# Score products of differential attention: the lo part of the queries laid on both halves of the rows

## The chip, the cores and the metric

One Trainium2 chip (trn2), one of its cores. The metric is the device time of one execution in microseconds (us); lower is better. A measurement of this kernel gives the median of several runs.

## What is computed

The reference is a decoder layer over 1024 positions of 1024 channels. The change touches the scores of its first part, differential attention with 4 heads. Each head has two score sets (c = 0, 1) with 64 channels each, two softmaxes, and the difference of the two weighs the values:

```
sc = jnp.einsum("bhcqd,bhckd->bhcqk", q_blk, k).astype(jnp.float32) * scale
sc = jnp.where(mask, sc, -jnp.inf)
p = jax.nn.softmax(sc, axis=-1)
a = p[:, :, 0] - lam * p[:, :, 1]
return jnp.einsum("bhqk,bhkv->bhqv", a.astype(v.dtype), v)
```

Beside it run a convolution branch (width 31, LayerNorm, swish), cross-attention into 256 memory tokens and a gated feed-forward part with its own convolution.

## The kernel before, in words

TensorE multiplies in fp32r, a rounded form of float32. To keep the precision of float32 each operand is split into hi (rounded) and lo (the rest), and a product is made of several: `mm3` (lines 198 to 200) does hi x lo, lo x hi and hi x hi, on 128 rows each.

The stages follow each other: input projection, attention, output projection, cross-attention, feed-forward part. In the attention stage the score products have only 64 channels to sum over. So the kernel lays K by 128 rows: `ks[c]` holds the hi part of the keys of set c on one half of the rows and the lo part on the other half. `qd[c]` holds the hi part of the queries on both halves, so one product of 128 rows gives q_hi x k_hi + q_hi x k_lo. The lo part of the queries, `ql`, holds set 0 on rows 0 to 63 and set 1 on rows 64 to 127; one product of 64 rows gives q_lo x k_hi. The term q_lo x k_lo is left out.

`qk_split` (line 667 on) makes these tiles once per head. It casts K and Q to hi on ScalarE and subtracts for lo on VectorE (lines 220 and 221 in `split`), and the puts (`put`, line 676) copy halves of rows to where they belong. Every put is a transfer of 64 rows x 4 KB from SBUF to SBUF, issued on the queue of SyncE (SP), which also issues the loads of weights (line 171) and the stores of memory keys and values (`kv_dr`, lines 635 and 655). Of a head's tiles the first `nq` come from pool Q (8 tiles), the rest from pool R (26 tiles).

The attention loop goes over 32 units, four heads with eight query blocks of 128 in the order `QBS = [7, 0, 6, 1, 5, 2, 4, 3]`. A unit of query block qb has (qb + 1) x 128 keys. Up to 512 keys (small unit) both sets go into one PSUM tile, and the scores of both stand together; above that (large unit) each set is a part of its own with a PSUM tile of its own, cut into pieces of at most 512 columns. After the products of a part comes the mask product (line 705). Then VectorE takes the row maximum (line 715), ScalarE the exponential (line 721), VectorE combines the two sets (lines 741 to 745); two steps later TensorE transposes (line 759), four steps later it weighs the values (line 772). Between these, TensorE works on products of the memory keys and values (`mm3` with 256 columns), the filler. VectorE also works through the convolution (line 371).

TensorE's order is the order in which the program is written (`manual_schedule`), and it works through it in order. The order of the other engines and of SP's queue comes from a scheduler that plans with its own costs. `qk_split` of head h + 1 is appended after step 4 of head h, and the casts come in step 5:

```
            if step % 8 == 4 and step < 24:
                lanes.append(qk_split(step // 8 + 1))
```

The first head is split before the loop.

Of the kernel before, what the change touches and what calls it, by code (L numbers as in the profile page):

```python
# [10 lines left out]
F32R = mybir.dt.float32r  # L11
# [46 lines left out]
def hybrid_block_kernel(ctx: ExitStack, tc: tile.TileContext, xT, memT, pos, vecs, lams, ropec,  # L58
                        wi, wv, wo, wq, wkv, wc, wu, wd, gfin, outT, outB):
    nc = tc.nc  # L60
# [15 lines left out]
    def nm(s):  # L76
        cnt[0] += 1
        return f"{s}_{cnt[0]}"

    def R():  # L80
        return pt.tile([P, S], F32R, tag="t", name=nm("r"))

    def Q(dt=F32):
        return pq.tile([P, S], dt, tag="q", name=nm("q"))
# [4 lines left out]
    def BIG():  # L89
        return big[0].tile([P, S], F32, tag="big", name=nm("big"))  # L90
# [16 lines left out]
    def f(ap):  # L107
        return ap.bitcast(F32)
# [76 lines left out]
    def need(kind, m, ahead=None):  # L185
        if ahead is None:
            ahead = 1
        load_to(index[(kind, m)] + ahead)
        return prepped.pop((kind, m))
# [15 lines left out]
    def bs(b):  # L205
        return slice(b * P, (b + 1) * P)

    def proj(w, xs, ks=None, kmajor=True):

        ks = list(range(KT)) if ks is None else list(ks)  # L210
        ps = BIG()
        loops = [(k, h) for k in ks for h in range(2)] if kmajor else [(k, h) for h in range(2) for k in ks]
        for k, h in loops:
            mm3(ps[:, hs(h)], (w[0][:, bs(k)], w[1][:, bs(k)]), xs(k, h), k == ks[0], k == ks[-1])
        return ps

    def split(src, hi, lo, scale=None):

        if scale is None:
            nc.scalar.copy(out=hi, in_=src)  # L220
            nc.vector.tensor_tensor(out=lo, in0=src, in1=f(hi), op=ALU.subtract)  # L221
        else:
            nc.scalar.mul(hi, src, scale)
            nc.vector.scalar_tensor_tensor(out=lo, in0=src, scalar=scale, in1=f(hi), op0=ALU.mult, op1=ALU.subtract)
# [262 lines left out]
    qk = [None] * 8  # L487
# [22 lines left out]
    with tc.manual_schedule(engines={mybir.EngineType.PE}):  # L510
        w, w2 = need("in", 12), need("in", 8, 0)
        ps, ps2 = BIG(), BIG()
# [26 lines left out]
    for m in in_order[3:]:  # L539
        w = need("in", m)  # L540
        ps = proj(w, xs_in)
# [125 lines left out]
    def qk_split(h):  # L667


        nq = (0, 2, 2, 4)[h]  # L670
        t = [Q(F32R) if i < nq else R() for i in range(5)]
        ks, qd, ql = t[:2], t[2:4], t[4]
        rows = (slice(0, 64), slice(64, P))

        def put(dst, src):
            nc.sync.dma_start(out=f(dst), in_=f(src))

        kh, kl = R(), R()
        split(qk[4 + h], kh, kl)
        for c in range(2):  # L680
            put(ks[c][rows[c]], kh[rows[c]])
            put(ks[c][rows[1 - c]], kl[rows[c]])
        yield
        qh = R()
        split(qk[h], qh, ql)
        for c in range(2):
            put(qd[c][rows[0]], qh[rows[c]])
            put(qd[c][rows[1]], qh[rows[c]])
        yield
        hl[h] = ks, qd, ql  # L690

    def scores(u, cs):

        h, qb = u["h"], u["qb"]
        nk = (qb + 1) * P
        ks, qd, ql = hl[h]
        cuts = [0, 384, 640] if nk == 640 else [*range(0, nk, HALF), nk]
        for n0, n1 in zip(cuts, cuts[1:]):
            for c in cs:
                rows = slice(64 * c, 64 * c + 64)  # L700
                nc.tensor.matmul(u["ps"][c][:, n0:n1], ql[rows, bs(qb)], ks[c][rows, n0:n1], start=True, stop=False)  # L701
            for c in cs:
                nc.tensor.matmul(u["ps"][c][:, n0:n1], qd[c][:, bs(qb)], ks[c][:, n0:n1], start=False, stop=n1 < nk)  # L703
        for c in cs:
            nc.tensor.matmul(u["ps"][c][:, nk - P:nk], identb, maskb, start=False, stop=True)
# [18 lines left out]
    def start_unit(h, qb):  # L724
        nk = (qb + 1) * P
        if (h, qb // 4) not in s0:
            s0[(h, qb // 4)] = small(4, "s0", 4)
        u = {"h": h, "qb": qb, "sums": small(2, "sums", 6), "nmx": small(2, "nmx", 6)}
        if nk <= HALF:
            both = BIG()  # L730
            t = T()
            u.update(both=both, ps=[both[:, hs(0)], both[:, hs(1)]], p=[t[:, :nk], t[:, HALF:HALF + nk]])
        else:
            u.update(both=None, ps=[None, None], p=[None, None])
        return u
# [172 lines left out]
    for _ in qk_split(0):  # L908
        pass
    with tc.manual_schedule(engines={mybir.EngineType.PE}):  # L910
# [3 lines left out]
        for step in range(n + LW):  # L914
# [4 lines left out]
            u = None  # L919
            if step < n:  # L920
                u = start_unit(*plan[step])
                units.append(u)
                if u["both"] is not None:
                    scores(u, (0, 1))
                    maxima(u, None)
                else:
                    u["ps"][0] = span(u)
                    scores(u, (0,))
                    maxima(u, 0)
# [16 lines left out]
            if u and u["both"] is None:  # L946
                u["ps"][1] = span(u)
                scores(u, (1,))
                maxima(u, 1)
                u["p"][1] = T()[:, :(u["qb"] + 1) * P]  # L950
                expo(u, 1)
# [4 lines left out]
            if step % 8 == 4 and step < 24:  # L956
                lanes.append(qk_split(step // 8 + 1))
# [37 lines left out]
    for m in range(8):  # L995
        res = Q()
        nc.scalar.dma_start(out=res, in_=xT[bs(m), :])
        if m < 2:
            ps = two[m]
        else:  # L1000
            ps = proj(need("out", m), xs_out)
# [190 lines left out]
    for m in range(8):  # L1192
        ps = proj(need("co", m), xs_co) if m > 1 else co[m]
# [401 lines left out]
```

## Time and profile before

| what | before |
|---|---|
| median of 3 runs | 1430.73 us (1429.91 to 1436.02) |
| the profiled execution | 1430.6 us |
| its span | 1428.7 us |
| PE busy | 1398.4 us (98%) |
| DVE (VectorE) busy | 1059.6 us (74%) |
| ACT (ScalarE) busy | 570.6 us (40%) |
| POOL (GpSimd) busy | 200.5 us (14%) |

The span is what the profile covers of an execution; the rest lies around it. PE is TensorE's products, PEld its weight loads, which may run beside products. A product's record is longer than its share of the array, since products follow each other in a pipeline: the distance from start to start tells what one costs, not its length. SPq is SP's queue; a row there is the time of issuing a transfer, not of the transfer.

### The profile page before, as it was taken

What the parts mean: (1) busy time and instruction counts of PE and PEld (TensorE: products, weight loads), DVE (VectorE), ACT (ScalarE), POOL (GpSimd) and SP (SyncE); (2) the same over time, 40 slices, a digit from 0 to 9 for tenths busy, and PEclk for the clock granted to TensorE, in tenths of its full rate; (3) what the DMA queues carried; (4) which work ended last, traced back from release to release, by engine and by line L of the source; (5) the groups of instructions that cost most, each with busy time, mean ns of one, the idle gap of its engine ahead of it and who ended that gap; (6) DMA issues with size and microseconds to landing.
All of it is one profiled execution on the core that took longest, in us unless ns stands there. A gap on an engine that the chain in (4) does not pass through costs nothing.

```text
span 1428.7 us, 17463 instructions
## 1 busy us (share of the span) xinstructions
PE 1398.4 (98%) x6709; PEld 1148.1 (80%) x6709; DVE 1059.6 (74%) x1377; ACT 570.6 (40%) x1015; POOL 200.5 (14%) x169
## 2 busy tenths in 40 slices
PE   9999999999999999999989999999999989999998
PEld 6888887778777888888878888788888878888886
DVE  7899998878855424454688888888888887656636
ACT  6211224667773223343464443444443442211213
POOL 0000000013110000000114234343334400000000
PEclk9999999999999999999999999999999999999999
DMA  6142135523405421112431222222222274323103
GB/s 230 34 103 63 56 103 144 159 83 103 119 31 171 163 101 59 63 42 74 148 111 59 74 74 89 79 84 74 89 75 89 89 308 163 108 70 118 44 1 118
DMA packets 51620, 141.55 MB, mean 99 GB/s; under 512 B 6608, under 2 KB 8912, under 8 KB 51536
## 3 DMA queue, kind: packets, MB, share of 16 engines
q1 hardware_dynamic: 45040, 123.65, 26.1%
q10 hardware_dynamic: 6496, 16.78, 3.7%
q8 instruction: 53, 0.87, 0.3%
q14 instruction: 31, 0.25, 0.1%
HBM read 101.51 MB, written 28.41 MB: 91 GB/s over the span
## 4 chain that ended last, share of the span: by engine, by line
PE 65%; DVE 15%; issue 7%; ACT 7%; POOL 4%; DMA 2%; SPq 0%; POOLq 0%; ACTq 0%; DVEq 0%
PE big L198 15%; PE big L199 15%; PE big L200 15%; DVE q L1323 4%; POOL t L1178 4%; ACT q L1321 3%; PE big L703 2%; PE tb L772 2%; PE big L701 2%; PE bk L198 1%; PE bk L200 1%; PE bk L199 1%; DVE wu L221 1%; DVE q L1342 1%; PE mb L198 1%
## 5 line engine op out<-in xcount | busy, mean ns | idle before, releaser
L199 PE MATMUL big<-r,wlo 128*128 128x512 f32 x624 | 243.2, 390 | 0.6 <-DVE wlo L182 0.6
L200 PE MATMUL big<-r,whi 128*128 128x512 f32 x624 | 243.0, 389 | 0.0
L198 PE MATMUL big<-r,whi 128*128 128x512 f32 x560 | 219.0, 391 | 2.0 <-DVE r L304 1.0
L181 ACT CAST whi<-raw 128x1024 fp32r<-128x1024 f32 x58 | 61.3, 1056 | 205.2 <-PE big L200 169.6
L199 PEld LDWEIGHTS big<-r,wlo 128*128 128x128 f32 x624 | 117.2, 188 | 24.7 <-DVE wlo L182 0.9
L200 PEld LDWEIGHTS big<-r,whi 128*128 128x128 f32 x624 | 117.2, 188 | 24.5
L1427 DVE TENSOR_TENSOR t<-t,big 128x1024 f32<-128x1024 f32 x70 | 85.3, 1219 | 62.1 <-PE big L200 62.0
L1323 DVE SCALAR_TENSOR_TENSOR q<-q,vec,q 128x1023 f32<-128x1023 f32 x88 | 112.5, 1280 | 20.5 <-ACT q L1321 20.4
L198 PEld LDWEIGHTS big<-r,whi 128*128 128x128 f32 x560 | 105.2, 188 | 25.3 <-DVE r L304 1.9
L198 PE MATMUL big<-r,r 128*128 128x512 f32 x312 | 121.8, 390 | 0.3 <-DVE t L1427 0.3
L199 PE MATMUL big<-r,r 128*128 128x512 f32 x312 | 121.5, 390 | 0.0
L200 PE MATMUL big<-r,r 128*128 128x512 f32 x312 | 121.5, 389 | 0.0
L198 PE MATMUL ub<-r,wu 128*128 128x512 f32 x302 | 118.6, 393 | 1.2 <-ACT half L1278 1.2
L200 PE MATMUL ub<-r,wu 128*128 128x512 f32 x302 | 117.6, 389 | 0.0
L199 PE MATMUL ub<-r,wu 128*128 128x512 f32 x302 | 117.6, 389 | 0.0
L1178 POOL TENSOR_TENSOR t<-uraw 128x512 f32<-128x512 f32 x22 | 48.6, 2210 | 387.7 <-DMA uraw<-in_wu_dram 166.9
L198 PE MATMUL ub<-r,t 128*128 128x512 f32 x228 | 91.2, 400 | 9.5 <-ACT half L1278 4.8
L199 PE MATMUL ub<-r,t 128*128 128x512 f32 x228 | 90.2, 396 | 0.0
L200 PE MATMUL ub<-r,t 128*128 128x512 f32 x228 | 90.0, 395 | 0.0
L371 DVE SCALAR_TENSOR_TENSOR cv<-t,vec,cv 128x511 f32<-128x511 f32 (+14 forms) x120 | 83.8, 739 | 0.0
L181 ACT CAST r<-raw 128x1024 fp32r<-128x1024 f32 x22 | 23.0, 1049 | 135.4 <-PE big L198 134.7
L182 DVE TENSOR_TENSOR wlo<-raw,whi 128x1024 fp32r<-128x1024 f32 x58 | 70.7, 1220 | 4.8 <-ACT whi L181 4.7
(333 smaller groups left out, 3010.5 us busy)
## 6 DMA issues: line engine op xcount, KB each, us to landing
uraw<-in_wu_dram SPq DMA_DIRECT2D x88, 256.0 KB, 2.9
z_dr<-q SPq DMA_DIRECT2D x22, 512.0 KB, 2.6
raw<-in_wd_dram SPq DMA_DIRECT2D x22, 512.0 KB, 3.7
t<-z_dr SPq DMA_DIRECT2D x22, 512.0 KB, 4.6
raw<-in_wkv_dram SPq DMA_DIRECT2D x16, 512.0 KB, 3.7
raw<-in_wi_dram SPq DMA_DIRECT2D x14, 512.0 KB, 3.6
r<-r SPq DMA_DIRECT2D x16, 256.0 KB, 6.1
kv_dr<-r SPq DMA_DIRECT2D x8, 512.0 KB, 3.5
```

The lines of the kernel that those rows point to most:

```text
L181: nc.scalar.copy(out=hi, in_=raw)
L182: nc.vector.tensor_tensor(out=lo, in0=raw, in1=f(hi), op=ALU.subtract)
L198: nc.tensor.matmul(out, wh, xl, start=start, stop=False, **kw)
L199: nc.tensor.matmul(out, wl, xh, start=False, stop=False, **kw)
L200: nc.tensor.matmul(out, wh, xh, start=False, stop=stop, **kw)
L371: nc.vector.scalar_tensor_tensor(out=y[:, i:], in0=x[:, :n2 - i], scalar=t, in1=y[:, i:], op0=ALU.mult, op1=ALU.add)
L701: nc.tensor.matmul(u["ps"][c][:, n0:n1], ql[rows, bs(qb)], ks[c][rows, n0:n1], start=True, stop=False)
L703: nc.tensor.matmul(u["ps"][c][:, n0:n1], qd[c][:, bs(qb)], ks[c][:, n0:n1], start=False, stop=n1 < nk)
L1178: nc.gpsimd.tensor_tensor(out=out, in0=a, in1=b, op=ALU.add)
L1321: nc.scalar.mul(t, u, tp[2])
L1323: nc.vector.scalar_tensor_tensor(out=t[:, d:], in0=u[:, :S - d], scalar=tp[2 - d], in1=t[:, d:], op0=ALU.mult, op1=ALU.add)
L1427: nc.vector.tensor_tensor(out=h2[m], in0=h2[m], in1=ps, op=ALU.add)
```

## The change

`ql` becomes two tiles like `qd`: `ql[c]` holds the lo part of the queries of set c on both halves of the rows. The lo part is first computed into a tile of its own, `qlo`, and four more puts per head copy it. All score products take 128 rows, so the lo product now gives q_lo x k_hi + q_lo x k_lo. In small units the lo and the hi product of set 0 stand ahead of those of set 1, where the two lo products stood first.

```diff
         nq = (0, 2, 2, 4)[h]
-        t = [Q(F32R) if i < nq else R() for i in range(5)]
-        ks, qd, ql = t[:2], t[2:4], t[4]
+        t = [Q(F32R) if i < nq else R() for i in range(6)]
+        ks, qd, ql = t[:2], t[2:4], t[4:]
...
-        qh = R()
-        split(qk[h], qh, ql)
+        qh, qlo = R(), R()
+        split(qk[h], qh, qlo)
         for c in range(2):
-            put(qd[c][rows[0]], qh[rows[c]])
-            put(qd[c][rows[1]], qh[rows[c]])
+            for r in rows:
+                put(qd[c][r], qh[rows[c]])
+                put(ql[c][r], qlo[rows[c]])
...
             for c in cs:
-                rows = slice(64 * c, 64 * c + 64)
-                nc.tensor.matmul(u["ps"][c][:, n0:n1], ql[rows, bs(qb)], ks[c][rows, n0:n1], start=True, stop=False)
-            for c in cs:
+                nc.tensor.matmul(u["ps"][c][:, n0:n1], ql[c][:, bs(qb)], ks[c][:, n0:n1], start=True, stop=False)
                 nc.tensor.matmul(u["ps"][c][:, n0:n1], qd[c][:, bs(qb)], ks[c][:, n0:n1], start=False, stop=n1 < nk)
```

In the new file the lo product is line 701, the hi product line 702 and the mask product line 704; later lines move up by one.

What the scheduler makes of it stands in the order of the programs. SP's queue at head 0, before: `r_1761` and `r_1762` are ks, `r_1763` and `r_1764` are qd of set 0 and 1, `raw` is a weight load.

```order
L676 DMA r_1761<-r_1766 64x1024
L676 DMA r_1762<-r_1766 64x1024
L676 DMA r_1761<-r_1767 64x1024
L676 DMA r_1762<-r_1767 64x1024
L676 DMA r_1763<-r_1774 64x1024 x2
L676 DMA r_1764<-r_1774 64x1024 x2
L171 DMA raw_1904<-in_wkv_dram 128x1024
```

The same place in the new program; `r_1765` and `r_1766` are ql of set 0 and 1.

```order
L676 DMA r_1761<-r_1767 64x1024
L676 DMA r_1762<-r_1767 64x1024
L676 DMA r_1761<-r_1768 64x1024
L676 DMA r_1762<-r_1768 64x1024
L676 DMA r_1763<-r_1775 64x1024 x2
L171 DMA raw_1910<-in_wkv_dram 128x1024
L676 DMA r_1765<-r_1776 64x1024 x2
L676 DMA r_1764<-r_1775 64x1024
L676 DMA r_1766<-r_1776 64x1024
L676 DMA r_1764<-r_1775 64x1024
L676 DMA r_1766<-r_1776 64x1024
L171 DMA raw_1967<-in_wkv_dram 128x1024
```

Four puts are added, and one weight load now stands between qd and ql of set 0. In heads 1 and 2 the order is the same from the second put of qd of set 0 on.

SP's queue at head 3, before: `q_3383` and `q_3384` are ks, `q_3385` and `q_3386` are qd.

```order
L676 DMA q_3383<-r_3388 64x1024
L655 DMA kv_dr<-r_2839 128x1024
L676 DMA q_3384<-r_3388 64x1024
L676 DMA q_3385<-r_3416 64x1024
L676 DMA q_3383<-r_3389 64x1024
L676 DMA q_3384<-r_3389 64x1024
L676 DMA q_3385<-r_3416 64x1024
L676 DMA q_3386<-r_3416 64x1024 x2
L171 DMA raw_4185<-in_wo_dram 128x1024
```

The same place in the new program; `q_3403` and `q_3404` are qd, `r_3405` and `r_3406` are ql.

```order
L676 DMA q_3401<-r_3407 64x1024
L676 DMA q_3402<-r_3407 64x1024
L655 DMA kv_dr<-r_2857 128x1024
L676 DMA q_3403<-r_3435 64x1024
L676 DMA q_3401<-r_3408 64x1024
L676 DMA q_3402<-r_3408 64x1024
L676 DMA q_3403<-r_3435 64x1024
L676 DMA q_3404<-r_3435 64x1024 x2
L676 DMA r_3405<-r_3436 64x1024 x2
L676 DMA r_3406<-r_3436 64x1024 x2
L171 DMA raw_4209<-in_wo_dram 128x1024
```

Here all puts of ql stand behind those of qd. On PE the order of the products is the same but for the small units, where L701 of set 1 now stands behind the hi product of set 0.

## Rows read from the trace of the kernel before

**Rows 1.** Busy time by stretch: the attention stage (us, PE, PEld, DVE, ACT, POOL, PEclk).

```profile
236.90:410.00 173.10, 166.31 (x1095) 130.13 (x1095) 140.67 (x272) 119.96 (x321) 25.97 (x55) 1.00 0.40 117
```

**Rows 2.** Waits, 228 to 412 us, of DVE and SP: total us, times, longest.

```profile
DVE s L715 <- PE big L705: 28.0, 29, 2.6
...
SPq L171 <- DVE wlo L182: 52.1, 8, 20.2
```

**Rows 3.** PE in order of time at head 1's first part: start us, us.

```profile
288.52 0.28 PE L199 MATMUL mb<-r,wlo 128*128 128x256 f32 x1
288.64 0.28 PE L200 MATMUL mb<-r,whi 128*128 128x256 f32 x1
288.85 0.49 PE L701 MATMUL big<-q,r 64*128 64x512 f32 x1
289.27 0.50 PE L703 MATMUL big<-q,r 128*128 128x512 f32 x1
...
290.48 0.23 PE L705 MATMUL big<-maskb,identb 128*128 128x128 bf16 x1
```

**Rows 4.** PE in order of time in the value projection, products of 512 columns.

```profile
225.68 0.39 PE L199 MATMUL bk<-whi,r 128*128 128x512 f32 x1
225.90 0.39 PE L200 MATMUL bk<-whi,r 128*128 128x512 f32 x1
```

**Rows 5.** PE in order of time, a small unit of 128 keys in head 1.

```profile
295.08 0.33 PE L701 MATMUL big<-q,r 64*128 64x128 f32 x2
...
295.62 0.29 PE L705 MATMUL big<-maskb,identb 128*128 128x128 bf16 x2
```

**Rows 6.** The last two puts (L676) of heads 0 to 3 on SP: issue, landing.

```profile
L676 SPq DMA_DIRECT2D r<-r x2: 913/1031/1149, 234.1 to 235.1; - x2
...
DMA to landing us min/median/max: 6.0/6.1/6.2
...
L676 SPq DMA_DIRECT2D r<-r x2: 891/1197/1503, 281.6 to 283.2; - x2
...
DMA to landing us min/median/max: 6.1/6.3/6.4
...
L676 SPq DMA_DIRECT2D r<-r x2: 556/811/1066, 325.5 to 326.2; - x2
...
DMA to landing us min/median/max: 6.4/6.4/6.4
...
L676 SPq DMA_DIRECT2D q<-r x2: 622/744/867, 372.5 to 373.2; - x2
...
DMA to landing us min/median/max: 4.8/5.1/5.3
```

**Rows 7.** PE in order of time: first products of the first two parts of the heads.

```profile
239.00 0.50 PE L703 MATMUL big<-r,r 128*128 128x512 f32 x1 [1.59 <-DMA r<-r]
...
242.56 0.50 PE L701 MATMUL big<-r,r 64*128 64x512 f32 x1
...
293.18 0.49 PE L701 MATMUL big<-q,r 64*128 64x512 f32 x1
...
331.72 0.50 PE L701 MATMUL big<-q,r 64*128 64x512 f32 x1
...
335.76 0.50 PE L701 MATMUL big<-q,r 64*128 64x512 f32 x1
...
376.25 0.49 PE L701 MATMUL big<-q,r 64*128 64x512 f32 x1
...
379.87 0.49 PE L701 MATMUL big<-q,r 64*128 64x512 f32 x1
```

**Rows 8.** Busy time by stretch around two idle spells of PE, columns as in rows 1.

```profile
739.10:743.30 4.20, 4.17 (x10) 3.30 (x11) 4.01 (x4) 2.93 (x6) 2.97 (x2) 0.50 0.18 64
1161.50:1165.70 4.20, 0.07 (x1) 0.00 (x0) 4.13 (x6) 2.77 (x3) 0.00 (x0) 1.00 1.03 417
1166.60:1170.00 3.40, 3.40 (x10) 2.62 (x9) 3.36 (x3) 2.72 (x3) 0.00 (x0) 0.50 1.03 411
```

## The prediction

> **What bounds the kernel now.** I read the table of stretches first, then TensorE (PE) in order of time, then the puts and the waits. The attention stage takes 173.1 us of the span, with PE busy 166.3 us and VectorE 140.7 [rows 1]. PE's instructions stand in a fixed order, so this stage ends when PE has gone through them; VectorE idles 32 us in it, and 28.0 us of that is the row maximum (L715) waiting for score products [rows 1, 2].
>
> Busy does not mean at full rate. In the timeline of one score part (head 1, 1024 keys, four products of 512 columns) the reader is to see starts: L701 to L703 takes 0.42 us, and first L701 to mask product (L705) 1.63 us for four products [rows 3]. Products of the same 512 columns that use all 128 rows one after another start 0.22 to 0.23 us apart elsewhere [rows 4]. So each change between 64 rows (L701) and 128 rows (L703) costs some 0.2 us. The change into the first L701 shows too: it comes 0.21 us after a product of 256 columns, where such products follow each other after 0.12 [rows 3].
>
> **What the change removes.** With 128 rows everywhere no product changes the row count. A part of 1024 keys took 0.21 + 1.63 = 1.84 us and takes 0.12 + 4 x 0.227 = 1.03: 0.8 saved. The surplus hangs on the changes, not on the columns, so I take 0.8 for all 32 large parts (4 heads, 4 query blocks, 2 score sets): 25.6 us. The 16 small units (up to 512 keys) gain little: there the two 64-row products run side by side, two of 128 columns together in 0.33 us [rows 5], and this overlap is lost. The one shown takes 0.54 + 0.21 now and 4 x 0.12 + 0.12 then, 0.15 saved; I take 0.2 each, 3.2 us (bounds 0 and 0.3). Together PE saves **28.8 us**, 7.2 in each head. No instruction is added on PE, ScalarE or VectorE; the added lo x lo terms ride in rows that were empty.
>
> A rule of the Trainium skill speaks against this: its page TensorE: Matmul & The Clock Gate (Part 3: Packing small matmuls — row/col tiling) says that a weight load overlaps a running product only when it goes to other rows of the array. By it no 128-row product could hide its load and the large parts would gain nothing. The row contradicts it, products of 128 rows with new weights at 0.227 us [rows 4]; by the rule the 25.6 us would be nothing, and it is a rival below.
>
> **What the change adds.** Four transfers per head (L676, 64 rows x 4 KB), all on SP's one queue, and all behind the split of the queries. The first part of a head now needs its two ql puts as well as its two qd puts. In the order of heads 0 to 2, a weight load, then ql of set 0, then the four puts of set 1 stand behind qd of set 0; in head 3 ql stands behind all qd. So ql of set 0 is complete one transfer after the last put of the old kernel (two in head 3), and ql of set 1 four transfers later (two in head 3).
>
> The old last puts landed at 241.3, 289.3, 332.6 and 378.5 us (issue plus landing: 235.1 + 6.2, 283.2 + 6.1, 326.2 + 6.4, 373.2 + 5.3), each 0.7 to 1.3 after the put before it [rows 6]. I take **1.1 us a transfer** (bounds: 0.55, were two halves to travel together, and 1.35). The weight load of 512 KB isn't priced apart in a row; I take the same, bounds 0.55 and 2.2. That puts ql of set 0 at 242.4, 290.4, 333.7 and 380.7.
>
> Old starts of the first parts: 238.6 effectively (the L703 at 239.00 had waited 1.59 for puts, less 0.42), 288.85, 331.72, 376.25 [rows 3, 7]. PE must wait for every head. How long follows from a chain: the puts of head h+1 start when the split in step 5 of head h is cast, behind six large parts and three small ones (6 x 0.8 + 3 x 0.2 = 5.4 us saved by then); the last 1.8 us saved before a head begins only lengthen its wait.
> - Head 0: starts 3.8 late. The second part followed the first by 242.56 - 238.6 = 4.0 us, now 3.2, but its puts come 4.4 after the first's: 1.2 more. At the cast: 3.8 + 1.2 - 5.4 = 0.4 early.
> - Head 1: ql at 290.4 - 0.4 = 290.0; PE is there at 288.85 - 0.4 - 1.8 = 286.65: **waits 3.35**. Start 1.15 late; second part (4.33 apart, now 3.5) 0.9 more; at the cast 3.4 early.
> - Head 2: ql at 330.3, PE at 326.5: **waits 3.8**; start 1.4 early; second part 1.2 more; at the cast 5.6 early.
> - Head 3: ql at 375.1, PE at 368.85: **waits 6.2**; start 1.2 early; the second part (3.6 apart, now 2.8) needn't wait, its puts come 2.2 after. Then 7.2 saved: 8.4 early.
>
> So of 28.8 us some 20 go into waits and 8.4 stay. Two costs come off.
> (a) PE's clock. After 4.2 us without work the granted clock was 0.50, 1.2 of 2.4 GHz, for 3.4 us; and after another such spell 10 products took 4.2 us at 0.50, which is 10 x 0.227 = 2.3 at full clock [rows 4, 8]. So about 1.8 us per wait that long. The new waits are 5.5 (head 0: 242.4 less 236.9, the start of the old first product, 0.5 + 1.59 before 239.00), 3.35, 3.8 and 6.2. In heads 0 to 2 the wait of the second part swallows 1.2, 0.9, 1.2 of it. All four: 0.6 + 0.9 + 0.6 + 1.8 = 3.9; only the longest two: 2.4. I take 3.2.
> (b) VectorE. Its 32 us of idleness cover 8.4, but between a head's start and the cast PE runs 5.4 us faster, against a fourth of 32, so some maxima will come late: bounds 0 and 5, I take 2.
> The SP queue delays the later loads of weights by four transfers, 4.4 us; PE waits there for nothing new, since each head now starts later than its puts. If that cover fails, the fill products (L198) wait.
>
> **Sum:** 28.8 - 20.4 - 3.2 - 2.0 = 3.2 us gained. The profiled execution took 1430.6 us (span 1428.7 and 1.9 around it), 0.1 from the median of the runs: **1427.4 us**, no change that a measurement can tell (0.5%, 7.2 us: below 1423.6 or above 1437.9).
>
> **Rivals.**
> *The puts travel faster (faster).* Each put touches half of the rows, so two might move together, 0.55 us a transfer. Then no second part waits, and the chain gives 3.3 late, 2.1 early at the cast, 1.1 early, 6.5, 5.1, 10.5, 7.2 and 14.4 us early at the end: with 4 us for clock and VectorE 1420. Were all waits gone but head 0's (5.0), it would be 28.8 - 5.0 - 2 = 21.8 less, 1409. For it: in one head the last two landed 0.7 apart [rows 6]. Against it: in the four places the landings keep the spacing taken above [rows 6].
> *A blocked SP queue (slower).* A weight load now stands ahead of the ql puts, and such loads (L171) wait for VectorE to release the buffer: 52.1 us in 8 waits, 6.5 each, the longest 20.2 [rows 2]. A load that waits holds all puts behind it, and PE waits one for one. If that takes 6.5 us in two heads, 1427.4 + 13 = 1440. It decides from 10 us of lateness on. Against it: in the old run PE waited for puts in one place alone, 1.59 us in head 0 [rows 7].
> *Weight loads stay exposed (slower).* This is the rule above, made a mechanism: a 128-row product with new query weights still starts 0.42 us after the last. Large parts gain nothing, small ones lose the overlap, at most one product of 0.42 each (6.7 us; I take 5), and the heads start late by 3.8 + 0.4, 1.55 + 0.1, 2.0 + 0.4 and 4.45: 12.7. Together 1430.6 + 17.7 = 1448. The products that follow each other after 0.227 us speak against it [rows 4].
> *It does nothing visible:* the surplus is no matter of rows, and the waits hide in it: 1431.
>
> **How the numbers follow.** Forecast 0.57; faster puts 0.26; blocked queue 0.09; exposed loads 0.05; nothing 0.03. So faster 0.26, same 0.60, slower 0.14. The forecast's own range: without (b) and with the small clock term 1424.6; with 5 us of (b), all of the clock and 1.35 us a transfer 1435. To hold 8 in 10 the range reaches into the faster puts and half of the blocked queue: 1413 to 1440.
>
> **What would show it.** In the profile after: starts of the four products 0.22 to 0.23 apart and a part of 1024 keys at about 0.95 us; no pair of L701 side by side; PE waiting for DMA on ql (L701) in all four heads, some 3 to 6 us, most in head 3; a granted clock of 0.50 behind at least two of them; VectorE's waits for the mask product shorter inside the heads. I'm wrong if PE doesn't wait in heads 1 to 3 (then 1420 or less), if products stay 0.42 apart, or if an L171 load on SP waits ahead of the ql puts.

## The result and the profile after

| what | before | after |
|---|---|---|
| median of 10 runs each, taken side by side | 1432.28 us (1428.33 to 1437.13) | 1439.63 us (1438.07 to 1442.5) |
| the profiled execution, its span | 1430.6, 1428.7 us | 1440.0, 1438.2 us |

The ratio is 1.0056 [1.0041, 1.0071]: the changed kernel is about 8 us **slower**. The forecast was 1427.4 us, 3.2 us less than before and too little to be seen; the change went the other way.

The head of the page of the changed kernel shows that PE has 14 us less busy time than the 1398.4 us of before, and the span is still 9.5 us longer:

```profile
span 1438.2 us, 17505 instructions
## 1 busy us (share of the span) xinstructions
PE 1384.2 (96%) x6709; PEld 1155.2 (80%) x6709; DVE 1059.5 (74%) x1377; ACT 570.9 (40%) x1015; POOL 202.4 (14%) x169
```

So the loss is time in which PE stands still, and the first question is where. The table of stretches of the changed kernel (columns as in [rows 1], the last two being DMA share and GB/s) has the attention stage, from its last product ahead of the scores to its last mask product, in the first row. Below it stand two of the waits at the start of a head (0 and 1) and the four stretches after such waits at a granted clock of 0.50:

```profile
236.70:416.29 179.59, 148.32 (x1079) 133.84 (x1078) 138.95 (x268) 118.19 (x315) 27.84 (x54) 0.94 0.50 136
237.00:242.94 5.94, 0.01 (x2) 0.03 (x1) 3.74 (x5) 1.56 (x2) 0.00 (x0) 0.87 1.03 262
242.94:248.21 5.27, 5.27 (x20) 4.55 (x21) 1.88 (x2) 1.21 (x2) 0.00 (x0) 0.50 1.02 266
291.10:295.18 4.08, 0.00 (x0) 0.02 (x1) 1.23 (x4) 2.01 (x5) 0.70 (x1) 1.00 1.03 227
295.99:299.40 3.41, 3.41 (x17) 3.06 (x16) 2.36 (x2) 1.22 (x3) 0.00 (x0) 0.50 0.86 172
340.37:343.78 3.41, 3.41 (x18) 3.41 (x18) 2.22 (x2) 1.97 (x6) 0.00 (x0) 0.50 0.50 149
386.14:391.57 5.43, 5.43 (x22) 4.71 (x22) 1.23 (x1) 0.55 (x4) 0.00 (x0) 0.50 0.44 118
```

The same stage of before:

```profile
236.70:407.95 171.25, 164.46 (x1079) 128.16 (x1078) 138.86 (x267) 118.33 (x315) 25.87 (x54) 1.00 0.41 118
```

PE does the same 1079 products in both. The stage took 171.2 us and takes 179.6, at a mean clock of 0.94 where it was 1.00. (8.3 of the 9.5 us of the span lie here. Most of the other 1.2 comes up outside the change, near 1170 us, where the clock is at half for 6.8 us instead of the 3.4 in [rows 8].)

PE in order of time at head 0 shows both halves of the story (in brackets: how long PE stood still before a product, and what ended that). The first part starts after a wait and runs at half clock, with starts 0.43 apart; the second part, at full clock, has the 0.23 that was forecast:

```profile
242.94 0.77 PE L701 MATMUL big<-r,r 128*128 128x512 f32 x1 [5.93 <-issue]
243.50 0.63 PE L702 MATMUL big<-r,r 128*128 128x512 f32 x1
243.93 0.63 PE L701 MATMUL big<-r,r 128*128 128x512 f32 x1
244.36 0.63 PE L702 MATMUL big<-r,r 128*128 128x512 f32 x1
...
248.57 0.40 PE L701 MATMUL big<-r,r 128*128 128x512 f32 x1
248.81 0.40 PE L702 MATMUL big<-r,r 128*128 128x512 f32 x1
249.04 0.39 PE L701 MATMUL big<-r,r 128*128 128x512 f32 x1
249.27 0.40 PE L702 MATMUL big<-r,r 128*128 128x512 f32 x1
249.51 0.23 PE L704 MATMUL big<-maskb,identb 128*128 128x128 bf16 x1
...
295.19 0.47 PE L701 MATMUL big<-q,r 128*128 128x512 f32 x1 [4.13 <-DMA r<-r]
...
338.95 0.47 PE L701 MATMUL big<-q,r 128*128 128x512 f32 x1 [3.65 <-issue]
...
386.14 0.77 PE L701 MATMUL big<-q,r 128*128 128x512 f32 x1 [4.58 <-DMA r<-r]
```

The four first products of the heads wait 5.93, 4.13, 3.65 and 4.58 us, 18.3 in all; before there was one such wait of 1.59 [rows 7]. Two are put down to "issue", which means that the profile shows nothing that released them, and two to the DMA; by their place in the program all four need the same puts. The table of waits, from 228 us to the stage's end, counts them so (total us, times, longest), and shows what else PE waits for:

```profile
PE big L701 <- issue: 9.6, 2, 5.9
PE big L701 <- DMA r<-r: 8.7, 2, 4.6
PE mb L198 <- DVE half L628: 3.0, 3, 1.3
PE big L701 <- ACT t L720: 2.8, 5, 1.0
PE tb L828 <- DVE r L224: 2.3, 2, 1.2
PE tb L758 <- ACT t L759: 1.7, 2, 1.3
```

In the kernel before, the waits of L701 for the exponential (L720, which holds the PSUM tile) and of the transposes for the copies of L759 did not show.

**The stage, added up.** I took every distance from one PE start to the next in the trace, took off the gap where PE stood still (the waits), and half of what lay at a granted clock of 0.50 (the loss to the clock); the rest is work at full clock. In us:

| kernel | stage | work | waits | lost to half clock |
|---|---|---|---|---|
| before | 171.2 | 164.5 | 6.8 | 0 |
| after | 179.6 | 139.5 | 31.3 | 8.8 |
| difference | +8.3 | -24.9 | +24.5 | +8.8 |

The saving is real, and it is spent on waits and on the clock. Of the 24.5 us of new waits, 16.7 (18.3 less 1.6) are the four head starts.

### The profile page after: what moved, and what is told of

Same layout as the page of the kernel before. It is cut to its first block, busy times and chain, and to the rows that moved or that the text cites. A ratio compares the mean times of both kernels' runs of the same rounds, so it can differ in the third digit from the quotient of the medians.

```text
span 1438.2 us, 17505 instructions
## 1 busy us (share of the span) xinstructions
PE 1384.2 (96%) x6709; PEld 1155.2 (80%) x6709; DVE 1059.5 (74%) x1377; ACT 570.9 (40%) x1015; POOL 202.4 (14%) x169
## 4 chain that ended last, share of the span: by engine, by line
PE 60%; DVE 16%; ACT 8%; issue 7%; POOL 5%; DMA 3%; SPq 1%; POOLq 0%; ACTq 0%; DVEq 0%
PE big L198 15%; PE big L199 15%; PE big L200 15%; POOL t L1177 4%; DVE q L1322 4%; ACT q L1320 3%; DMA r<-r 2%; PE tb L771 2%; PE bk L198 1%; DVE wu L221 1%; PE bk L200 1%; PE bk L199 1%; DVE q L1341 1%; PE ub L198 1%; PE ub L199 1%
## 5 line engine op out<-in xcount | busy, mean ns | idle before, releaser
L1322 DVE SCALAR_TENSOR_TENSOR q<-q,vec,q 128x1023 f32<-128x1023 f32 x88 | 112.6, 1281 | 20.5 <-ACT q L1320 20.4
```

The lines of the kernel that those rows point to most:

```text
L1322: nc.vector.scalar_tensor_tensor(out=t[:, d:], in0=u[:, :S - d], scalar=tp[2 - d], in1=t[:, d:], op0=ALU.mult, op1=ALU.add)
```

## The experiments

**The two halves of the change apart.** First the product on 128 rows without the added puts, on the kernel before:

```diff
-                rows = slice(64 * c, 64 * c + 64)
-                nc.tensor.matmul(u["ps"][c][:, n0:n1], ql[rows, bs(qb)], ks[c][rows, n0:n1], start=True, stop=False)
-            for c in cs:
+                nc.tensor.matmul(u["ps"][c][:, n0:n1], ql[:, bs(qb)], ks[c][:, n0:n1], start=True, stop=False)
```

> The old kernel's tiles and puts (one ql tile, lo of set 0 on rows 0 to 63 and of set 1 on rows 64 to 127), but the lo product takes all 128 rows of it, so it adds a stray term, lo of the other set's queries times lo of the keys, in place of the lo x lo term. It has the saving without the puts. Theory 1: all 28.8 us less some us for late maxima, no wait for puts but the old 1.6 in head 0, no half clock in the stage: 1403 to 1410 us. Theory 2: VectorE and ScalarE bound the stage, less than half of 28.8 arrives: 1418 us or more.

Measured: 1412.48 us, ratio 0.9865 [0.9846, 0.9883], 18 to 19 us faster than before. Its stage in the table of stretches:

```profile
238.21:390.22 152.01, 140.55 (x1079) 127.54 (x1078) 137.70 (x267) 117.04 (x315) 25.72 (x54) 0.99 0.45 133
```

PE in order of time, the second pair of products of head 1's first part, 0.23 us apart:

```profile
286.82 0.40 PE L700 MATMUL big<-q,r 128*128 128x512 f32 x1
287.05 0.40 PE L701 MATMUL big<-q,r 128*128 128x512 f32 x1
```

The work is 138.8 us, as in the changed kernel, with 11.5 us of waits and 1.7 lost to the clock. The first theory holds in the main; the time is 2 us above its range, since waits grew by 4.7 us. 1.5 us of them are a second wait for puts, at head 3, which the theory did not have.

Then the added puts without the saving: the changed kernel with its lo product on 64 rows again (`ql[c][rows, ...]`, `ks[c][rows, ...]`, both lo products first).

> The changed kernel's tiles and puts, but the lo product on 64 rows as before (rows of its own set of ql, the order of products as before). It has the cost of the change without its saving; lo x lo is left out as before. Theory 1: PE comes to the head starts later, so it waits less than in the changed kernel, but 3.8 + 1.6 + 2.0 + 4.5 us late at the four starts, and the clock may fall in some: 1432 + 12 to 18 = 1444 to 1450 us. Theory 2: the slack takes it up, within 5 us of before, 1432 to 1437.

Measured: 1453.09 us, ratio 1.0156 [1.0141, 1.017], somewhat above the first theory's range. The work is 164.3 us, so nothing is saved; waits are 20.6 us and the clock loses 9.7. PE's largest wait in it is now for the puts:

```profile
PE big L702 <- DMA r<-r: 14.7, 5, 5.2
```

The two ratios answer the main question: 128 rows alone are worth 1.35%, the added puts alone cost 1.56%. The sum is +0.2%, with some 0.25 of uncertainty; both together measure +0.56%. So the parts nearly add up; the 0.35% between them, 5 us with an uncertainty of some 4, is what they do to each other. One thing the pair doesn't part: with the added puts a head takes two more tiles from pool R, the pool into which the exponentials and the copies of the transposes write too. In the changed kernel ScalarE waits 4.0 us in the stage for puts and a store that still use such a tile; before, and with 128 rows and no puts, it never does. So "the added puts" means here the puts with their tiles.

**Splitting a head earlier.** If the puts are late by a few us, starting them two steps earlier should hide them:

```diff
-            if step % 8 == 4 and step < 24:
+            if step % 8 == 2 and step < 24:
```

> The changed kernel with one number changed: the split of the next head is appended after step 2 of a head instead of step 4, so that its puts start some 10 us earlier. Theory 1 (PE waits for the ql puts at the head starts, and each wait halves the clock): the waits of heads 1 to 3 (4.13 + 3.65 + 4.58 = 12.4 us in the trace after) go, with them three stretches at half clock (3.4 + 3.4 + 5.4 = 12.2 us, worth 6.1); head 0 stays. 1439.6 - 18.5 = about 1421 us. Theory 2 (VectorE and ScalarE can't follow the shorter products, the waits only show their slack): the waits go to other places, at least 1434 us. Theory 3 (the added puts hold up other transfers): no gain, or slower than 1439.

Measured: 1438.32 us, ratio 1.006 [1.0043, 1.0078], far from the 1421 expected. The put waits of heads 1 to 3 are gone, as foreseen, but head 0 waits 7.01 us, and a new wait of the same size stands inside head 0. ScalarE at that place, in order of time:

```profile
281.89 0.90 ACT L720 ACTIVATE t<-big,s 128x768 f32<-128x768 f32 x1 [4.34 <-DMA q<-r]
```

And PE:

```profile
287.02 0.58 PE L198 MATMUL mb<-r,whi 128*128 128x256 f32 x1 [7.02 <-DVE half L628]
```

The exponential waits 4.34 us for a put that still uses the tile it is to write, and 5 us later a filler product waits 7.02 us for VectorE. With two heads' tiles alive for longer the tiles run short: in the stage ScalarE waits 16.1 us for puts that still use a tile, where it was 4.0 us for puts and a store, and 9.2 us are lost to half clock. The run doesn't separate the theories: it trades one wait for another.

**Keeping PE busy while it waits.** To test the clock alone, 14 products of constants that nothing reads were put ahead of each head's first scores:

```diff
+                    if step % 8 == 0:
+                        wb = TB()
+                        for _ in range(14):
+                            nc.tensor.matmul(wb, warm[:, :P], warm, start=True, stop=True)
```

> The changed kernel with 14 dummy products (bf16, 128 rows, 512 columns, some 3 us) ahead of the first scores of each head, into a PSUM tile that nobody reads, so that PE isn't idle while the ql puts travel. Theory 1 with the clock as a cost of its own: the granted clock stays at 1.0 in the stage, the 17.5 us at half clock in the trace after are worth 8.8, of which nothing was swallowed: about 1431 us. If the half clock lies in time that is waited anyway: 1438 to 1440 us.

Measured: 1439.74 us, ratio 1.0063 [1.005, 1.0076], the time of the second case. As a test of the whole it is inconclusive: the dummies took 3.1 us a head at full clock, once waited themselves for a PSUM tile (at head 2), and at heads 0 and 3 ended before the puts landed, so the clock still lost 7.3 us of the 8.8:

```profile
PE tb L929 <- ACT t L759: 4.3, 1, 4.3
```

Heads 1 and 2 show something all the same. PE's wait for the puts was 0.32 us at head 1 and none at head 2, where the half clock fell into the dummies, and behind both starts the clock stayed at 1.00. From the first product of the head to the next head's first put (columns as in [rows 1]):

```profile
294.91:321.86 26.95, 25.33 (x200) 23.21 (x201) 20.45 (x42) 19.30 (x58) 4.91 (x11) 1.00 0.28 90
342.21:372.43 30.22, 28.69 (x227) 26.18 (x225) 24.41 (x54) 23.67 (x68) 10.99 (x20) 1.00 0.07 22
```

The changed kernel takes 27.9 and 31.8 us for the same, at 0.94 and 0.95. So the half clock makes these stretches longer. The 1.0 and 1.6 us gained did not last: from that put to the next head's start it took 20.4 and 16.1 us where the changed kernel takes 15.9 and 15.4.

**Filling the waits with real work.** The filler was moved to the head starts, with smaller shares after each unit:

```diff
-    T0, T1, TS = 4.5, 3.25, 8
+    T0, T1, TS = 3.9, 2.7, 8
...
+            if step < n and step % 8 == 0:
+                fill(4.5)
```

> The changed kernel with its filler moved: 4.5 us more of the products of memory keys and values are written ahead of the first scores of each head, and less after each unit (shares of 3.9 and 2.7 us a unit where 4.5 and 3.25 stood). No product is added, and the twelve puts of a head stay. Theory 1 (the loss is TensorE standing still at the four head starts, 18.3 us, and the half clock behind that, 8.8 us): of each wait some 4 us are filled with work that is done later now, and the clock holds, so the put waits fall to below 6 us and the stretches at half clock to at most two; the products taken from inside the heads are missed there a little (VectorE sets the pace in part, 3 to 6 us): 1415 to 1424. Theory 2 (the splits and puts set the pace of a head, and TensorE merely waits at another place): each head gets shorter ahead of the next split no more than before, the waits come back inside the heads or at the next head's start, and the time stays at 1434 to 1441.

Measured: 1441.93 us, ratio 1.0057 [1.0042, 1.0072], against the first theory and 1 us above the second's range. PE's largest wait in it:

```profile
PE big L701 <- DMA r<-r: 16.9, 4, 7.8
```

The put waits came back, 16.9 us of them: 7.76 us at head 1, where 4.13 stood, 5.74 at head 3, 0.54 at head 2, and 2.90 at the second part of head 0. From the first product of one head to that of the next it takes 51.9, 46.4 and 48.9 us; in the changed kernel 52.3, 43.8 and 47.2. Filling a head's start doesn't shorten the loop that begins there: the first units, the casts of the next head's K and Q, twelve puts one after the other, the next head's first product. The test is not clean, though. Between the start of head 1 and the next head's first put PE did 225 products where the changed kernel has 200, so the split also came later in the order of the work, and the stretch grew from 27.9 to 34.0 us.

**Fewer puts.** Each half of a split was written straight to where it belongs, so that six puts a head remain of twelve; the lo x lo term stays in:

```diff
-        kh, kl = R(), R()
-        split(qk[4 + h], kh, kl)
+        kl = R()
         for c in range(2):
-            put(ks[c][rows[c]], kh[rows[c]])
-            put(ks[c][rows[1 - c]], kl[rows[c]])
+            r, o = rows[c], rows[1 - c]
+            split(qk[4 + h][r], ks[c][r], kl[r])
+            put(ks[c][o], kl[r])
...
-            for r in rows:
-                put(qd[c][r], qh[rows[c]])
-                put(ql[c][r], qlo[rows[c]])
+            r, o = rows[c], rows[1 - c]
+            split(qk[h][r], qd[c][r], ql[c][r])
+            put(qd[c][o], qd[c][r])
+            put(ql[c][o], ql[c][r])
```

> The changed kernel with 6 puts per head instead of 12: the splits write each 64-row half of hi and lo straight into the half of ks, qd and ql where the same rows lie, and only the other halves are put (and the hi part is put from there). Same products, lo x lo included. It adds two casts (1.04 us each) on ScalarE and two subtractions (1.2 us) on VectorE per head. Theory 1 (the puts' chain at the head starts is the loss): ql of set 0 is complete with the fourth transfer instead of the ninth, PE waits at no head start for more than 1 us and the clock stays at 1.0 but perhaps in head 0; as with 128 rows and no puts (1412), plus some of the 10 us of added VectorE work: 1412 to 1420 us. Theory 2 (the loss of the change is contention with other work, whatever the number of puts): above 1430 us.

Measured: 1423.43 us, ratio 0.9946 [0.993, 0.9962]: 3 us above the first theory's range and 7 below the second's. The starts of heads 1 to 3 wait 0.8 us together, so the first theory holds in its mechanism. (The run also takes three tiles of pool R fewer a head.) What is left is head 0, whose split is late, and the clock behind it:

```profile
242.62 0.77 PE L700 MATMUL big<-r,r 128*128 128x512 f32 x1 [5.15 <-DVE cv L371]
243.19 0.63 PE L701 MATMUL big<-r,r 128*128 128x512 f32 x1
```

The same direct writing on the two kernels with 64 and with 128 rows in the lo product and one tile `ql` (four puts a head) shows what it costs by itself.

> The control: the old kernel (one ql tile, lo product on 64 rows) with the same writing of halves, 4 puts per head instead of 8. PE waited only 1.6 us for puts in the old kernel, so theory 1 gives no more than that: 1429 to 1433 us. If fewer puts by themselves made the kernel faster, 1425 us or less.

> The kernel with 128 rows and one ql tile (a stray term, lo of the other set's queries times lo of the keys, in place of lo x lo) with the same writing of halves, 4 puts per head. Theory 1: the 1.7 us waited in head 0 and its half clock (1.7 us) go, the added work on VectorE gives some back: 1408 to 1414 us.

Measured: 1440.6 us, ratio 1.0064 [1.0047, 1.0081], and 1417.41 us, ratio 0.9894 [0.9874, 0.9913]. Both miss their expectation upwards. Halving the tiles isn't free: a cast of 64 rows takes as long as one of 128, so the splits of a head take twice the instructions, and PE's waits grow by 5 us in each. So the gain of six puts over twelve comes in spite of this cost. ScalarE's casts in the kernel with six puts:

```profile
278.30 1.04 ACT L220 CAST q<-q 64x1024 fp32r<-64x1024 f32 x1
```

and in the changed kernel:

```profile
277.16 1.07 ACT L220 CAST r<-q 128x1024 fp32r<-128x1024 f32 x1
```

**Fewer puts, and filler ahead of head 0** (four shares of 2.6 us ahead of the loop where two stood: `for _ in range(4): fill(2.6)`):

> The kernel with six puts per head and the lo x lo term, with 5.2 us more filler ahead of head 0 (four shares of 2.6 us where two stood). Theory 1 (its remaining loss is the wait of 5.15 us at head 0 and 3.4 us of half clock behind it): the wait is filled, 1414 to 1419. Theory 2 (head 0 is late because of VectorE and ScalarE, which the filler's evictions hold up further): no gain, 1421 to 1426.

Measured: 1417.89 us, ratio 0.9895 [0.988, 0.9911]: as the first theory said, and 1% faster than before with the lo x lo term computed. The table of stretches from 236.70 us to its last mask product, then the longest wait of the filler ahead of head 0 and the stretch behind it:

```profile
236.70:396.44 159.74, 142.36 (x1087) 128.60 (x1085) 147.92 (x277) 123.43 (x321) 28.36 (x54) 0.99 0.40 117
237.82:240.73 2.91, 0.00 (x1) 0.01 (x1) 2.88 (x5) 2.11 (x3) 0.00 (x0) 1.00 1.04 225
240.73:244.20 3.47, 3.47 (x29) 3.47 (x30) 3.44 (x5) 0.85 (x2) 0.00 (x0) 1.00 1.01 282
```

PE in order of time at head 0, whose first product doesn't wait:

```profile
246.59 0.40 PE L700 MATMUL big<-r,r 128*128 128x512 f32 x1
```

From head to head it now takes 45.6, 39.0 and 39.6 us. The filler helps here, where only head 0 was late; why it helps here and not above is argued, not shown: the split of head 0 stands ahead of the loop, so that the filler doesn't put it off.

The same was tried on the fast kernel with one tile of lo queries (three shares instead of two):

> The kernel with one tile of lo queries, eight puts per head and 128 rows in the lo product (its stray term as said before), with 2.6 us more filler ahead of head 0. Theory 1 (a wait at head 0 of 1 to 2 us and the 1.7 us of half clock in its stage go): 1409 to 1412. Theory 2 (filler is only moved and nothing waits less): 1412 to 1414.

Measured: 1418.12 us, ratio 0.9894 [0.9877, 0.9911], slower than the 1412.48 without it. The put wait is gone, but waits on ScalarE and VectorE inside the stage take its place, 13.9 us in all against 11.5. The stage itself takes 152.2 us, as without the filler (152.0); it starts 4.6 us later, and there the time is lost. Why the filler costs that much ahead of the stage I didn't find out.

## Why the prediction was wrong

What was foreseen of the mechanism came: products of 128 rows follow each other after 0.23 us; PE waits for the puts at all four heads; the clock drops behind the waits; no weight load was held up on SP ahead of the `ql` puts. The rivals "weight loads stay exposed" and "the puts travel faster" are refuted, by the 0.23 us and by the waits. What failed is the sizing of the loop from one head's first product to the next: term (a), the half clock, nearly half of which the waits of the second parts were to swallow, and the weight load ahead of the `ql` puts, priced like a put. Term (b), the waits for other engines, and the saving were wrong too. In the terms of the sum:

| term | forecast, us | measured, us |
|---|---|---|
| saving on PE | 28.8 | 24.9 |
| waits at head starts beyond the old one, and of second parts | 20.4 | 16.7 (second parts 0) |
| (a) half clock | 3.2 | 8.8 |
| (b) other waits, on VectorE and ScalarE | 2.0 | 7.8 |
| sum, in the stage | 3.2 gained | 8.4 lost |

Against the forecast the other waits cost 5.8 us more, the clock 5.6 more, the saving is 3.9 smaller, and the waits for puts are 3.7 shorter. The rows hang together: time that PE loses inside a head it need not wait at the next start.

- **The saving.** The score products saved 21.1 us (58.6 to 37.5 for 192 of them), the transposes ahead of them 3.4. With the distance ahead of a part counted in, the 32 large parts saved 23.7 us where 25.6 were forecast, the 16 small units 2.1 where 3.2 were, and other products took 0.9 more. A large part saved 0.78 us, near the 0.8 taken from [rows 3], except the six that start behind a wait (the first ones of the heads and two later in head 3): 0.49 to 0.70 each.
- **The waits for puts** were sized well one by one: 5.5, 3.35, 3.8 and 6.2 forecast, 5.93, 4.13, 3.65 and 4.58 measured. At heads 1 to 3 that is luck in part: PE and the puts both came later than the chain has them, PE by 4.4, 8.8 and 12.7 us, the puts by 5.2, 8.6 and 11.0. The waits of the second parts, 1.2 us each, never came: their parts were late themselves, for the next reason.
- **(a) The clock.** I took 1.8 us a wait and let the second parts' waits swallow 0.9 to 1.2 of it in heads 0 to 2. It went the other way round: the half clock made the second parts late, so that they found their puts landed, and it was lost in full. After each of the four waits PE ran 3.4 to 5.4 us at 1.2 of 2.4 GHz, 17.5 us together, and half of that is lost. The Trainium skill (TensorE: Matmul & The Clock Gate, HAM oscillation) describes a kernel in which a wait for a DMA makes PE start every tile at the low clock, and counts half of the throttled time as lost. The trace agrees: four waits of four.
- **The loop.** From the first product of a head to that of the next it takes 52.3, 43.8 and 47.2 us, where the forecast's chain has 47.6, 40.3 and 44.8: 10.5 us more in all. About half comes up ahead of the next head's first put. Head 0 took 35.3 us from its start to there, where 32.7 were forecast (36.9 - 5.4 + 1.2); heads 1 and 2 took 27.9 for 26.9 and 31.8 for 29.9. The half clock in these three stretches is worth 2.6, 1.7 and 1.7 us; where the dummies kept the clock at 1.00, heads 1 and 2 took 26.95 and 30.22, as forecast. The last head, from its first product to its last mask product, saved 1.6 of 7.2 us; 2.7 of what is missing there is half clock.
- **From the first put to the next head's start** it took 16.9, 15.9 and 15.4 us, where the forecast had 14.9, 13.5 and 14.9: the other half. SP's queue at head 1, in order of time (start and length of the issues):

```profile
278.26 3.08 SPq L676 DMA_DIRECT2D q<-r  x4
281.45 0.65 SPq L676 DMA_DIRECT2D r<-r  x1
282.20 1.00 SPq L635 DMA_DIRECT2D kv_dr<-r  x1
283.25 1.52 SPq L676 DMA_DIRECT2D r<-r  x1
284.82 1.27 SPq L171 DMA_DIRECT2D raw<-in_wkv_dram  x1
286.19 6.38 SPq L676 DMA_DIRECT2D r<-r  x6
```

A store of memory keys and a weight load stand among the puts as foreseen, and the load is issued without a wait; the puts are issued 1.06 us apart (6.38 over 6), near the 1.1 taken. From issue to landing, the put issued at 283.25 and the load issued at 284.82 took:

```profile
DMA to landing us min/median/max: 5.3/5.3/5.3
DMA to landing us min/median/max: 7.9/7.9/7.9
```

So the load landed 4.1 us after the put ahead of it, at 292.7, and the `ql` puts behind that. In head 2 it was 2.7 us, in head 0 1.7; I had taken 1.1, with bounds of 0.55 and 2.2. In head 3, where no load stands there, the stretch is 0.5 us longer than forecast. That the load alone makes the rest is argued: no run moved it behind the puts.

- **(b) The other engines.** I foresaw that VectorE would be late inside the heads, and took 2 of 0 to 5 us. VectorE's wait for the mask product was to be shorter; it is 30.3 us in 17 waits where [rows 2] has 28.0 in 29:

```profile
DVE s L714 <- PE big L704: 30.3, 17, 4.3
```

Its longest waits, 4.30, 4.12 and 3.52 us, now stand at the first parts of heads 0, 1 and 3. There the idle time is of no use, and inside the heads PE waits for VectorE and ScalarE instead. Without the puts the same wait is 11.3 us in 16, and PE's waits for other things grow by 3.1 us, not 7.8: so 3.1 come with the shorter products and 4.7 with the puts and their tiles.

- **The chances.** "Slower" had 0.14, with a blocked queue as its main way. The slower side lay inside the forecast's own mechanism, in two terms that came out above the bounds I gave them: the clock (2.4 to 3.9 us) and the other engines (0 to 5).

The time saved in a head could reach the end only where the loop of split, puts and first products lets it. The forecast did see that loop, but it took its pace from the kernel before, at full clock and with a weight load at the price of a put.

## What to carry to other kernels

When an edit saves time on the engine that bounds a stage but makes an operand arrive later, follow the loop from that operand's first input to its next use, and charge what the wait itself causes (here the half clock) inside the loop. As long as the transfers set its length, what is saved elsewhere is waited away: with six puts instead of twelve, and filler ahead of head 0, 1.05% came through. Try the two halves of such a change apart first, since one alone was worth 1.35%.

## What the runs showed of the hardware beyond that

- **Copies of 64 rows within SBUF keep the DMA engines busy nearly twice as long per byte.** In the wait at head 1, where puts travel and the end of a weight load, the DMA share is 1.03 at 227 GB/s, by that 256 KB in 1.15 us; in [rows 8], where loads of 512 KB travel, the same share goes with 411 and 417 GB/s. So I estimate that four more puts a head take about 4.6 us of full DMA engines.
- **A change between 64 and 128 rows costs nearly as much as 512 columns.** It shows in the 21.1 us that the score products saved with the same columns. The Trainium skill (TensorEngine Tiling (Array Packing), Key Properties) says that a change of tiling mode drains the engine; the trace agrees in that each change costs time, with 0.42 against 0.23 us from start to start [rows 3, 4].
- **The length of a wait does not tell alone whether the clock drops.** The kernel with 128 rows and no puts stood still for 1.73 us at head 0 and then ran 3.41 us at 0.50 (its stretches below), while the six-put kernel with filler stood still for 2.91 us (its second row above) and kept 1.00:

```profile
238.72:240.45 1.73, 0.00 (x1) 0.00 (x0) 1.23 (x2) 1.37 (x2) 0.00 (x0) 1.00 1.02 227
241.64:245.05 3.41, 3.41 (x19) 3.41 (x18) 3.41 (x4) 1.21 (x2) 0.00 (x0) 0.50 0.73 273
```

Why the one kept the clock and the other didn't stays open.
